# GLA levels of a hybrid encoder: both directions side by side, one 512-column instruction for two of 256

## The chip, the cores and the metric

The kernel runs on one core of a Trainium2 chip. The metric is the device time of one execution in microseconds (us), as the median of several runs. Five engines work side by side, each through its own queue in order: PE multiplies matrices (PEld loads its weights), DVE, ACT and POOL work element by element on up to 128 partitions, and SP issues DMA transfers.

## The reference

One layer over a prompt of 512 tokens and a sample of 1024. The input projection feeds four mixers and a gate; the change touches the first mixer, gated linear attention (GLA), which runs in both directions over the tokens:

```python
def gla_chunked(q, k, v, g, strict):
    # o_t = sum_{s<=t (s<t if strict)} (q_t * prod_{r=s+1..t} a_r) . k_s  v_s
    ...
def gla_branch(q, k, v, lr, wg2_f, bg_f, wg2_b, bg_b, onorm_g):
    ...
    o_f = gla_chunked(q, k, v, log_gate(lr_f, wg2_f, bg_f), strict=False)
    o_b = flip(gla_chunked(flip(q), flip(k), flip(v), flip(log_gate(lr_b, wg2_b, bg_b)), strict=True))
    o = rms_norm(o_f + o_b, onorm_g)
def hybrid_layer(x, c, ...):
    h = rms_norm(x, pre_g) * (1 + scale[:, None, :]) + shift[:, None, :]
    proj = h @ w_in
    ...
    out_a = gla_branch(a_q, a_k, a_v, a_lr, ...)
    out_b = fnet_branch(b_u, fnet_w)
    out_c = attention_branch(c_q, c_k, c_v, q_norm_g, k_norm_g)
    out_d = sgu_branch(d_u, d_v, sgu_norm_g, sgu_w, sgu_b)
    mixed = jnp.concatenate([out_a, out_b, out_c, out_d], axis=-1) * jax.nn.silu(z)
    y = rms_norm(mixed @ w_out, post_g)
    return x + gate[:, None, :] * y
```

Here `a_r` is the forget gate, the exponential of `g`. There are 4 heads with 32 key columns and 64 value columns each.

## The kernel before

The tokens are handled in three groups of 512: group 2 is the prompt, groups 0 and 1 are the sample. All large matrix products take float32 values split into a high and a low part (`h` and `l`) and add three products (high by high, high by low, low by high), in the helper `mms` (L86). The split is always an ACT cast for the high part and a subtraction (L98) for the low one.

For each group GLA begins in `gla_in` (L711). The queries `aq` and keys `ak` lie as 128 rows (4 heads by 32) by 512 tokens. For each direction d a gate `f` of 128 by 512 is made: DVE L736, a POOL subtraction L98, an ACT exponential L738. Then `gla_pass1` (L762) works in seven levels, m = 1, 2, 4, ..., 64. Inside each block of 2m tokens, the level couples the one half's queries to the other half's keys: forward (`qpi`, `ksx`) the second half's queries to the first half's keys, backward (`qsi`, `kpx`) the other way round. Each level from m = 2 on splits half the columns of each of the four tiles, two pieces of 256 columns each into `kh`, `kl`, `qh`, `ql` (ACT L797 and L803, POOL L98 for `kl`, DVE L98 for `ql`), makes 48 small matmuls (L815, 32 rows by 128 columns), and takes the scores into `st` through a mask (DVE L820, `copy_predicated`). Behind that every level multiplies half the columns by the gate products of the half block: the two query halves on POOL, the two key halves on DVE (at m = 1 POOL multiplies the keys and DVE copies the other half, L841 and L842), and DVE forms the next level's gate products `ntf` and `ntb` out of pairs. The tile `st` is cleared by POOL (L785) before the first level writes it. The buffers `kh`, `kl`, `qh`, `ql` are double, so a level's operands can be ready one level ahead of PE.

The order of each engine's queue is set when the program is built, by a scheduler that simulates readiness and takes priorities. Wide matrix products of later stages (input projections of the other mixers) serve as filling work on PE. A level's first matmul is held back by hand until so many thousand columns of filling work are placed before it: `LEVEL_AT` (L42) gives, for each group, the start and the step, and L808 to L816 apply it. After the levels, `st` is split (`sth` on ACT L861, `stl` on DVE) and multiplied by the values.

Names of other stages that share the engines: `wt`, `wr`, `parts` are weights being split and passed through memory (L298, L306), `bev` (L953), `dvu` (L446), `kev` (L498) and `cev` (L507) are projections taken out of PSUM, `rp_t`, `rope` and the small `rs_` tiles (L124 to L134) belong to the norm and rotation of attention's queries and keys, `zr` is the gate path.

Of the kernel before, what the change touches and what calls it, by code (L numbers as in the profile page):

```python
# [39 lines left out]
LEVELS = (1, 2, 4, 8, 16, 32, 64)  # L40
# [5 lines left out]
def hybrid_encoder(  # L46
# [7 lines left out]
    V, S, G, T = nc.vector, nc.scalar, nc.gpsimd, nc.tensor  # L54
# [656 lines left out]
    def gla_in(pool, g, o4):  # L711

        aq = pool.tile([128, 512], F32, tag="aq", bufs=1, name="aq")
# [10 lines left out]
        lrT = pool.tile([96, 512], F32R, tag="qh", bufs=2, name="lrT")  # L724
        V.tensor_copy(lrT, lr)
        sub(V, lrT[32:64, :], lr[32:64, :], lrT[32:64, :])
        ff = []
        for d in range(2):
            pl = ps_s()
            T.matmul(pl, w2t[d], lrT, start=True, stop=True)  # L730
            t = pool.tile([128, 512], F32, tag="ql", bufs=2, name="gt_a")
            S.activation(t, pl, AF.Abs, bias=bg[:, d:d + 1])
            S.activation(t, t, AF.Exp, scale=-1.0)
            S.activation(t, t, AF.Ln, bias=1.0)
            f = pool.tile([128, 512], F32, tag=f"f{d}", bufs=1, name=f"f{d}")
# [15 lines left out]
        prod = pool.tile([128, 512], F32, tag="ksx", bufs=1, name="prod")  # L751
        mul(G, prod, aq, ak)
        pd = ps_o()
        for b in range(4):
# [6 lines left out]

    def gla_pass1(pool, ppool, g, blk0, ap_all, u_f, u_b, aq, ak, vhl, ff, avx):  # L762

        qpi = ppool.tile([128, 512], F32, tag=f"qpi{g}", bufs=1, name=f"qpi{g}")
        qsi = ppool.tile([128, 512], F32, tag=f"qsi{g}", bufs=1, name=f"qsi{g}")
        ksx = pool.tile([128, 512], F32, tag="ksx", bufs=1, name="ksx")
        mul(V, qpi, aq, ff[0])
        mul(V, qsi, aq, ff[1])

        prod = pool.tile([128, 512], F32, tag="kpx", bufs=1, name="prod2")  # L770
        for i, src in enumerate((qsi, qpi)):
            qv, kv, pv = (t.rearrange("p (n two) -> p two n", two=2) for t in (src, ak, prod))
            mul(G, pv[:, i], qv[:, i], kv[:, 1 - i])
# [9 lines left out]
        kpx = pool.tile([128, 512], F32, tag="kpx", bufs=1, name="kpx")  # L783
        st = pool.tile([128, 4, 4, 128], F32, tag="st", bufs=1, name="st")
        G.memset(st, 0.0)  # L785
        tf, tb = ff
        ntot = 512
        def halves(t, m):
            v = t.rearrange("p (n two m) -> p n two m", two=2, m=m)
            return v[:, :, 0, :], v[:, :, 1, :]  # L790

        def level(li, m):
            kh = pool.tile([128, 512], F32R, tag="kh", bufs=2, name="kh")
            kl = pool.tile([128, 512], F32R, tag="kl", bufs=2, name="kl")
            for i, src in enumerate((ksx, kpx)):
                s_, h_, l_ = halves(src, m)[i], halves(kh, m)[i], halves(kl, m)[i]
                S.copy(h_, s_)  # L797
                sub(G, l_, s_, h_)
            qh = pool.tile([128, 512], F32R, tag="qh", bufs=2, name="qh")
            ql = pool.tile([128, 512], F32R, tag="ql", bufs=2, name="ql")  # L800
            for i, src in enumerate((qsi, qpi)):
                s_, h_, l_ = halves(src, m)[i], halves(qh, m)[i], halves(ql, m)[i]
                S.copy(h_, s_)  # L803
                sub(V, l_, s_, h_)

            pts = [ps_s(), ps_s(), ps_s(), ps_o()]
            last = None
            at, step = LEVEL_AT[g]  # L808
            for i, (k, q) in enumerate(((kh, qh), (kh, ql), (kl, qh))):
                for b in range(4):  # L810
                    c = slice(b * 128, (b + 1) * 128)
                    for h in range(4):
                        r = slice(32 * h, 32 * h + 32)
                        with tc.issue_after(last.ins) if last is not None else after_columns(at + (li - 1) * step):
                            last = T.matmul(pts[h][:, c], k[r, c], q[r, c], start=i == 0 and b == 0, stop=i == 2,  # L815
                                            skip_group_check=True)  # L816
            for h in range(4):
                ptv = pts[h].rearrange("p (b t) -> p b t", b=4)
                if m < 64:
                    V.copy_predicated(st[:, h], mk[:, li - 1, :].unsqueeze(1).to_broadcast([128, 4, 128]), ptv)  # L820
                else:
                    S.copy(st[0:64, h, :, 64:128], ptv[0:64, :, 64:128])
                    S.copy(st[64:128, h, :, 0:64], ptv[64:128, :, 0:64])

        for li, m in enumerate(LEVELS):
            if m > 1:
                level(li, m)
            n2 = ntot // 2
            tfv, tbv = (t.rearrange("p (n two) -> p n two", two=2) for t in (tf, tb))

            def bc(t, i):
                return t[:, :, i].unsqueeze(2).to_broadcast([128, n2, m])

            q1, q2 = halves(qpi, m)
            mul(G, q2, q2, bc(tfv, 0))
            q1, q2 = halves(qsi, m)
            mul(G, q1, q1, bc(tbv, 1))
            if m == 1:
                k1, k2 = halves(ak, 1)
                mul(G, halves(ksx, 1)[0], k1, bc(tfv, 1))  # L840
                V.tensor_copy(halves(ksx, 1)[1], k2)  # L841
                V.tensor_copy(halves(kpx, 1)[0], k1)  # L842
                mul(G, halves(kpx, 1)[1], k2, bc(tbv, 0))
            else:
                k1, k2 = halves(ksx, m)
                mul(V, k1, k1, bc(tfv, 1))
                k1, k2 = halves(kpx, m)
                mul(V, k2, k2, bc(tbv, 0))
            ntf = pool.tile([128, n2], F32, tag=f"tf{n2}", bufs=1, name="ntf")
            ntb = pool.tile([128, n2], F32, tag=f"tb{n2}", bufs=1, name="ntb")  # L850
# [443 lines left out]
    with later():  # L1294
        t = [[], [], []]
# [110 lines left out]
```

## Time and profile before

| | |
|---|---|
| median of 3 runs | 1240.02 us (1235.35 to 1246.15) |
| the profiled execution | 1240.43 us, its span 1238.6 us |
| mean granted TensorE clock | 0.943 of full speed |
| busy, share of the span | PE 89%, DVE 61%, ACT 48%, POOL 31% |

The span is the stretch that the trace covers; the profiled execution's own time is 1.8 us longer. Times of single instructions below come from that execution. A row of the timeline reads: start, duration, engine, line, operation, output and inputs, shape, count, and in brackets the idle time of the engine just before it and what ended it.

### The profile page before, as it was taken

The numbers are of one execution on the slowest core, as the hardware profiler recorded it, in microseconds if no ns is written. First come the engines' busy times: TensorE is split into PE (matmuls) and PEld (weight loads), VectorE is DVE, ScalarE is ACT, GpSimd is POOL, SyncE is SP. The second block draws the span as 40 slices with busy tenths as digits, with TensorE's granted clock in tenths as the row PEclk, the third lists the DMA queues.
The fourth block names the chain that finished last, engine by engine and source line by source line (L and its number), as shares of the span: only waits on it lengthen the run. The fifth ranks groups of instructions, "written<-read, shape, count | busy, mean of one in ns | idle before, by whom it ended". The sixth has DMA issues, their size and how long they took to land. (4 is left out here: it accounts for less than half of the span.)

```text
span 1238.6 us, 21385 instructions
## 1 busy us (share of the span) xinstructions
PE 1105.1 (89%) x7906; PEld 973.3 (79%) x7906; DVE 754.5 (61%) x1440; ACT 597.3 (48%) x1472; POOL 382.0 (31%) x372
## 2 busy tenths in 40 slices
PE   5998779998999888998898899788989999988995
PEld 1587768764999886767898778588989998977995
DVE  6439776647454299552239852774787568686615
ACT  4334246643565235462123244444675667666623
POOL 3136654561011147113016510553141011223003
PEclk9999798998999998999999789789999999999998
DMA  8497656877433765576765346678347333264272
GB/s 316 159 324 243 227 183 202 309 271 234 150 117 116 239 198 159 173 251 199 250 203 168 112 147 194 197 252 282 128 145 247 111 103 94 81 212 130 82 252 97
DMA packets 126393, 233.99 MB, mean 189 GB/s; under 512 B 13092, under 2 KB 65796, under 8 KB 126288
## 3 DMA queue, kind: packets, MB, share of 16 engines
q1 hardware_dynamic: 121624, 227.49, 56.0%
q10 hardware_dynamic: 4664, 5.13, 1.2%
q8 instruction: 62, 1.02, 0.3%
q14 instruction: 43, 0.35, 0.1%
HBM read 162.97 MB, written 69.61 MB: 188 GB/s over the span
## 5 line engine op out<-in xcount | busy, mean ns | idle before, releaser
L86 PE MATMUL ps_mm<-wt,oph 128*128 128x256 f32 x2240 | 443.2, 293 | 20.7 <-DMA wt<-parts 11.0
L86 PEld LDWEIGHTS ps_mm<-wt,oph 128*128 128x128 f32 x2240 | 368.6, 199 | 30.6 <-DMA wt<-parts 11.3
L86 PE MATMUL ps_mm<-wt,opl 128*128 128x256 f32 x1120 | 326.0, 292 | 0.0
L86 PEld LDWEIGHTS ps_mm<-wt,opl 128*128 128x128 f32 x1120 | 222.0, 199 | 1.8
L86 PE MATMUL ps_mm<-oph,wt 128*128 128x512 f32 x576 | 194.8, 410 | 12.7 <-DMA wt<-parts 6.1
L554 DVE TENSOR_REDUCE nm<-ps_s 128x1 f32<-128x512 f32 x160 | 108.9, 686 | 58.6 <-PE ps_s L553 57.8
L86 PEld LDWEIGHTS ps_mm<-oph,wt 128*128 128x128 f32 x576 | 112.8, 197 | 38.9 <-ACT kh L797 3.8
L98 DVE TENSOR_TENSOR ptl<-ps_t,pth 128x512 fp32r<-128x512 f32 x160 | 108.4, 685 | 56.7 <-ACT pth L571 56.2
L98 POOL TENSOR_TENSOR wt<-wr,wt 128x512 fp32r<-128x512 f32 (+1 forms) x68 | 90.4, 1333 | 140.5 <-ACT wt L306 131.9
L571 ACT CAST pth<-ps_t 128x512 fp32r<-128x512 f32 x160 | 91.2, 590 | 65.8 <-PE ps_t L569 64.8
L561 ACT ACTIVATE pr<-ps_s,nm 128x512 f32<-128x512 f32 x160 | 109.5, 692 | 20.9 <-DVE nm L557 16.2
L86 PE MATMUL ps_mm<-opl,wt 128*128 128x512 f32 x288 | 117.9, 409 | 0.0
L569 PE MATMUL ps_t<-cs,pr 128*128 128x128 f32 x640 | 91.6, 276 | 1.1 <-DVE nm L557 0.6
L306 ACT CAST wt<-wr 128x512 fp32r<-128x512 f32 (+1 forms) x80 | 47.6, 597 | 77.5 <-PE ps_mm L86 36.0
L569 PEld LDWEIGHTS ps_t<-cs,pr 128*128 128x128 f32 x640 | 76.3, 143 | 9.5 <-PE ps_s L553 1.0
L101 POOL TENSOR_TENSOR oc<-oc,den 128x256 f32<-128x256 f32 x24 | 14.8, 629 | 220.3 <-DVE oc L104 199.0
L86 PEld LDWEIGHTS ps_mm<-opl,wt 128*128 128x128 f32 x288 | 56.7, 197 | 11.4
L552 PE MATMUL ps_s<-kT,qT 128*128 128x512 f32 x128 | 56.5, 442 | 5.0 <-ACT pr L561 4.8
L98 POOL TENSOR_TENSOR opl<-m,oph 128x512 fp32r<-128x512 f32 x30 | 39.1, 1319 | 52.6 <-ACT oph L1086 52.6
L553 PE MATMUL ps_s<-kT,qT 128*128 128x512 f32 x128 | 51.3, 401 | 0.0
L101 POOL TENSOR_TENSOR yt<-yt,gp 128x512 f32<-128x512 f32 x20 | 25.9, 1293 | 81.9 <-ACT jk L1118 64.8
L86 PE MATMUL ps_o<-pth,vkv 128*128 128x256 f32 x256 | 41.7, 285 | 0.6 <-DVE nm L557 0.6
(349 smaller groups left out, 2112.6 us busy)
## 6 DMA issues: line engine op xcount, KB each, us to landing
wt<-parts SPq DMA_DIRECT2D x136, 512.0 KB, 3.6
parts<-wt SPq DMA_DIRECT2D x68, 512.0 KB, 4.7
wr<-wp SPq DMA_DIRECT2D x48, 256.0 KB, 3.8
adar<-ada SPq DMA_DIRECT2D x16, 512.0 KB, 6.0
zT<-zr SPq DMA_DIRECT2D x30, 256.0 KB, 2.8
zt<-zT SPq DMA_DIRECT2D x30, 256.0 KB, 5.0
mt<-mixd SPq DMA_DIRECT2D x24, 256.0 KB, 5.2
wr<-wo SPq DMA_DIRECT2D x20, 256.0 KB, 4.5
```

Source lines behind the costliest of these rows:

```text
L86: t = T.matmul(out, a, b, start=first and i == 0, stop=last and i == len(terms) - 1, skip_group_check=skip)
L98: e.tensor_tensor(out, a, b, ALU.subtract)
L101: e.tensor_tensor(out, a, b, ALU.mult)
L306: (V.tensor_copy if part_engine(HIGH_V, u, S) is V else S.copy)(h, raw)
L552: T.matmul(sp, qT[:, h, qc], kT[kv][:, kc], start=True, stop=False)
L553: T.matmul(sp, qT[:, h, qc], kT[2 + kv][:, kc], start=False, stop=True)
L554: V.tensor_reduce(nm[:, f:f + 1], sp, AX, ALU.max, negate=True)
L561: S.activation(pr, sps[f], AF.Exp, bias=nm[:, 0:1], accum_out=rsum[:, b, h, f:f + 1])
L569: T.transpose(pt[:, k * 128:(k + 1) * 128], pr[f][:, k * 128:(k + 1) * 128], ident)
L571: S.copy(pth[f][:, :, qc], ptv)
```

## The change

Queries, keys and gates of both directions now lie side by side: `q2` and `k2` are tiles of 1152 columns (backward in the first 512, forward in the next), and `ff` holds three gate rows of 512 (backward, forward, backward again), for which ACT makes one exponential more per group. Views (`cross`, `pair`, `factor`) pick the halves of a level in both directions at once, so that each cast, subtraction and multiplication of a level is one instruction of 512 columns. The gate products of a level are one instruction of three rows. At m = 1 the keys are first copied in both directions by one ACT instruction of 1024 columns, and the multiplication of the keys moves from POOL to DVE. The first product of queries and gates becomes one DVE instruction of 1024 columns. `prod` gets a buffer of its own. The matmuls, `st`, and everything behind the levels stay.

```diff
-        ff = []
+        ff = pool.tile([128, 3, 512], F32, tag="ff", bufs=1, name="ff")
...
-            f = pool.tile([128, 512], F32, tag=f"f{d}", bufs=1, name=f"f{d}")
+            f = ff[:, 1 - d, :]
             V.tensor_scalar(f, pl, bg[:, d:d + 1], 0.0, ALU.add, ALU.min)
             sub(G, f, f, t)
+            if d:
+                S.activation(ff[:, 2, :], f, AF.Exp, scale=1.0 / 16.0)
             S.activation(f, f, AF.Exp, scale=1.0 / 16.0)
...
-        mul(V, qpi, aq, ff[0])
-        mul(V, qsi, aq, ff[1])
+        q2 = ppool.tile([128, pad], F32, tag=f"q2{g}", bufs=1, name=f"q2{g}")
+        k2 = pool.tile([128, pad], F32, tag="k2", bufs=1, name="k2")
+        qsi, qpi, ksx, kpx = q2[:, 0:512], q2[:, 512:1024], k2[:, 0:512], k2[:, 512:1024]
+        def cross(t, m):
+            v = t[:, 0:2 * (512 + m)].rearrange("p (i c) -> p i c", i=2)[:, :, 0:512]
+            return v.rearrange("p i (n two m) -> p i n two m", two=2, m=m)[:, :, :, 0, :]
+        def pair(t, m):
+            return t.rearrange("p (n two m) -> p two n m", two=2, m=m)
+        mul(V, q2[:, 0:1024].rearrange("p (i c) -> p i c", i=2), aq.unsqueeze(1).to_broadcast([128, 2, 512]), ff[:, 0:2, :])
...
+        S.copy(k2[:, 0:1024].rearrange("p (i c) -> p i c", i=2), ak.unsqueeze(1).to_broadcast([128, 2, 512]))
...
-            for i, src in enumerate((ksx, kpx)):
-                s_, h_, l_ = halves(src, m)[i], halves(kh, m)[i], halves(kl, m)[i]
-                S.copy(h_, s_)
-                sub(G, l_, s_, h_)
+            S.copy(pair(kh, m), cross(k2, m))
+            sub(G, pair(kl, m), cross(k2, m), pair(kh, m))
...
-            for i, src in enumerate((qsi, qpi)):
-                s_, h_, l_ = halves(src, m)[i], halves(qh, m)[i], halves(ql, m)[i]
-                S.copy(h_, s_)
-                sub(V, l_, s_, h_)
+            S.copy(pair(qh, m), cross(q2, m))
+            sub(V, pair(ql, m), cross(q2, m), pair(qh, m))
...
-            mul(G, q2, q2, bc(tfv, 0))
...
-            mul(G, q1, q1, bc(tbv, 1))
-            if m == 1:
-                mul(G, halves(ksx, 1)[0], k1, bc(tfv, 1))
-                V.tensor_copy(halves(ksx, 1)[1], k2)
-                V.tensor_copy(halves(kpx, 1)[0], k1)
-                mul(G, halves(kpx, 1)[1], k2, bc(tbv, 0))
...
-            mul(V, ntf, tfv[:, :, 0], tfv[:, :, 1])
-            mul(V, ntb, tbv[:, :, 0], tbv[:, :, 1])
+            mul(G, cross(q2, m), cross(q2, m), factor(0))
+            mul(V, cross(k2, m), cross(k2, m), factor(ntot))
+            mul(V, ng.rearrange("p (d n) -> p d n", d=3), gv[:, :, :, 0], gv[:, :, :, 1])
```

The queues are written anew by the scheduler. Three places are shown.

DVE at the start of group 2, before: the first product, the gate products of both directions in turn, the keys of m = 2 (`ksx`), and the other direction's keys (`kpx`) only behind them.

```order
L101 TENSOR_TENSOR qpi_4941<-aq,f_4904 128x512
L101 TENSOR_TENSOR ntf<-f_4904 128x256
L101 TENSOR_TENSOR qsi_4942<-aq,f_4914 128x512
...
L98 TENSOR_TENSOR ql<-qpi_4941,qh 128x128x2
L101 TENSOR_TENSOR ksx<-ksx,ntf 128x128x2
L101 TENSOR_TENSOR ntb<-ntb 128x4
L855 COPY tfin_5431<-ntf 128x4
L842 COPY kpx<-ak 128x256
L98 TENSOR_TENSOR ql<-qsi_4942,qh 128x128x2
L101 TENSOR_TENSOR av<-av,own_4954 128x1024
```

The same place after the change, where `k_4942` is the tile `k2` and `q_4941` the tile `q2`:

```order
L101 TENSOR_TENSOR k_4942<-k_4942,ff 128x2x256
L101 TENSOR_TENSOR q_4941<-aq,ff 128x1024
L101 TENSOR_TENSOR ng<-ff 128x768
L98 TENSOR_TENSOR wt<-wr,wt 128x512
L101 TENSOR_TENSOR ng<-ng 128x384
L101 TENSOR_TENSOR k_4942<-k_4942,ng 128x2x128x2
...
L845 COPY tfin_5375<-ng 128x8
L98 TENSOR_TENSOR ql<-q_4941,qh 128x2x128x2
```

The keys of both directions for m = 1 now come first of all, and those of m = 2 as the sixth instruction.

POOL at the same place, before, from the first multiplication of the keys to the low parts that level m = 2 needs:

```order
L101 TENSOR_TENSOR ksx<-ak,f_4904 128x256
L101 TENSOR_TENSOR prod_4946<-qpi_4941,ak 128x256
L101 TENSOR_TENSOR prod_4946<-qsi_4942,ak 128x256
L101 TENSOR_TENSOR qpi_4941<-qpi_4941,f_4904 128x256
L98 TENSOR_TENSOR kl<-ksx,kh 128x128x2
L101 TENSOR_TENSOR qsi_4942<-qsi_4942,f_4914 128x256
L101 TENSOR_TENSOR qpi_4941<-qpi_4941,ntf 128x128x2
L101 TENSOR_TENSOR kpx<-ak,f_4914 128x256
L98 TENSOR_TENSOR wt<-wr,wt 128x512
L101 TENSOR_TENSOR qsi_4942<-qsi_4942,ntb 128x128x2
L98 TENSOR_TENSOR kl<-ksx,kh 128x64x4
L98 TENSOR_TENSOR kl<-kpx,kh 128x128x2
```

And after:

```order
L98 TENSOR_TENSOR kl<-k_4942,kh 128x2x128x2
L101 TENSOR_TENSOR prod_4944<-q_4941,ak 128x256 x2
L101 TENSOR_TENSOR q_4941<-q_4941,ff 128x2x256
L98 TENSOR_TENSOR kl<-k_4942,kh 128x2x64x4
L98 TENSOR_TENSOR wt<-wr,wt 128x512 x2
```

The low part of the keys for m = 2, the last of twelve rows before, is the first now.

ACT at the start of group 1, before: the exponentials, two casts of `ksx`, then the copies of `kev`, and the query casts ahead of the second pair of them.

```order
L738 ACTIVATE f_8030<-f_8030 128x512
L738 ACTIVATE f_8040<-f_8040 128x512
L797 CAST kh<-ksx 128x128x2
L797 CAST kh<-ksx 128x64x4
L498 COPY kev<-ps_mm 128x256 x2
L397 ACTIVATE rp_t_4510<-kev 128x256
L803 CAST qh<-qpi_8067 128x128x2
L803 CAST qh<-qsi_8068 128x128x2
L498 COPY kev<-ps_mm 128x256 x2
```

And after, from the first key cast on:

```order
L802 CAST kh<-k_7954 128x2x128x2
L498 COPY kev<-ps_mm 128x256 x2
L397 ACTIVATE rp_t_4510<-kev 128x256
L802 CAST kh<-k_7954 128x2x64x4
L498 COPY kev<-ps_mm 128x256 x2
L124 ACTIVATE rs_l<-ropess,eps 128x4
L397 ACTIVATE rp_t_4548<-kev 128x256
L126 ACTIVATE rs_y<-rs_l 128x4
L124 ACTIVATE rs_l<-ropess,eps 128x4
L126 ACTIVATE rs_y<-rs_l 128x4
L806 CAST qh<-q_7953 128x2x128x2
```

The copies of `kev` now stand ahead of the second key cast, and the query cast stands behind the logarithms `rs_l`. On PE the order of the wide products is nearly the same; level m = 2 stands 1.5 thousand columns of filling work later than before in group 2, 6.7 thousand earlier in group 0, and 2.6 thousand later in group 1.

## Rows read from the trace of the kernel before

**Rows 1.** The page: engines over the whole span, and PE's 512-column matmuls (mean ns).

```profile
PE 1105.1 (89%) x7906; PEld 973.3 (79%) x7906; DVE 754.5 (61%) x1440; ACT 597.3 (48%) x1472; POOL 382.0 (31%) x372
...
L86 PE MATMUL ps_mm<-oph,wt 128*128 128x512 f32 x576 | 194.8, 410 | 12.7 <-DMA wt<-parts 6.1
```

**Rows 2.** Windows over the three GLA starts: busy time by engine, PE clock, DMA.

```profile
100.00:137.00 37.00, 24.74 (x196) 22.72 (x196) 35.51 (x56) 15.26 (x33) 28.65 (x26) 0.82 0.64 213
448.00:480.00 32.00, 22.87 (x160) 19.72 (x159) 31.79 (x57) 14.21 (x33) 25.70 (x23) 0.88 0.46 141
660.00:692.00 32.00, 26.09 (x236) 24.70 (x235) 29.79 (x61) 9.03 (x29) 23.46 (x27) 0.82 0.39 118
```

**Rows 3.** Timeline of PE, start of group 2: the instructions behind a wait.

```profile
121.62 0.33 PE L815 MATMUL ps_s<-qh,kh 32*128 32x128 f32 x3 [1.19 <-ACT kh L797]
...
126.97 0.48 PE L815 MATMUL ps_s<-qh,kl 32*128 32x128 f32 x3 [3.77 <-POOL kl L98]
...
133.31 0.51 PE L86 MATMUL ps_mm<-vhl,wsh 128*128 128x256 f32 x2 [1.79 <-ACT bev L953]
...
136.79 0.77 PE L86 MATMUL ps_mm<-wt,oph 128*128 128x256 f32 x2 [2.50 <-DVE dvu L446]
```

**Rows 4.** Timeline of PE, start of group 0: the instructions behind a wait.

```profile
464.57 0.47 PE L86 MATMUL ps_mm<-oph,wt 128*128 128x512 f32 x1 [3.79 <-DMA wt<-parts]
...
476.38 0.48 PE L815 MATMUL ps_s<-qh,kl 32*128 32x128 f32 x3 [3.19 <-POOL kl L98]
...
479.48 0.79 PE L86 MATMUL ps_mm<-oph,wt 128*128 128x512 f32 x1 [1.97 <-DVE zr L101]
```

**Rows 5.** Timeline of PE, start of group 1: the instructions behind a wait.

```profile
669.38 0.50 PE L86 MATMUL ps_mm<-wt,oph 128*128 128x256 f32 x2 [2.17 <-ACT kev L498]
...
683.72 0.43 PE L815 MATMUL ps_s<-qh,kh 32*128 32x128 f32 x1 [3.74 <-DVE st L820]
```

**Rows 6.** Timeline of POOL, group 2: the first low part of level m = 16.

```profile
141.84 0.74 POOL L98 TENSOR_TENSOR kl<-ksx,kh 128x256 fp32r<-128x256 f32 x1 [4.80 <-PE ps_o L815]
```

**Rows 7.** Groups by line and form, DVE and POOL (busy us, mean ns).

```profile
L98 DVE TENSOR_TENSOR ptl<-ps_t,pth 128x512 fp32r<-128x512 f32 x160 | 108.4, 685 | 56.7 <-ACT pth L571 56.2
L98 DVE TENSOR_TENSOR ql<-qpi,qh 128x256 fp32r<-128x256 f32 x18 | 7.4, 413 | 0.0
L101 DVE TENSOR_TENSOR ntf<-ntf 128x8 f32<-128x8 f32 x3 | 0.5, 158 | 0.0
...
L101 POOL TENSOR_TENSOR prod<-aq,ak 128x512 f32<-128x512 f32 x3 | 3.9, 1290 | 10.5 <-PE ps_mm L86 10.5
```

**Rows 8.** Timeline of ACT and POOL, group 2: last exponential, and the latest low part.

```profile
109.87 0.63 ACT L738 ACTIVATE f<-f 128x512 f32<-128x512 f32 x1 [0.92 <-POOL f L98]
...
125.10 1.81 POOL L98 TENSOR_TENSOR kl<-kpx,kh 128x256 fp32r<-128x256 f32 x1
```

**Rows 9.** Timeline of POOL and DVE, group 0: a small DVE instruction beside a long one.

```profile
445.70 2.56 POOL L98 TENSOR_TENSOR f<-f,gt_a 128x512 f32<-128x512 f32 x2 [11.24 <-ACT gt_a L734]
...
445.76 1.27 DVE L130 SCALAR_TENSOR_TENSOR rs_a<-rs_y 128x8 f32<-128x8 f32 x1
```

**Rows 10.** Timeline of SP, group 0: the DMA queue around the weights.

```profile
463.52 0.37 SPq L509 DMA_DIRECT2D qd<-cev  x1
463.98 5.52 SPq L298 DMA_DIRECT2D wt<-parts  x3
```

**Rows 11.** Timeline of ACT and POOL, group 1: the cast before `kev`, and clearing `st`.

```profile
668.38 0.40 ACT L797 CAST kh<-ksx 128x256 fp32r<-128x256 f32 x1 [5.88 <-DVE ksx L101]
...
677.93 1.81 POOL L785 MEMSET st<- 128x2048 f32 x1
```

**Rows 12.** Windows of 5 us behind the waits: columns as in Rows 2.

```profile
140.00:145.00 5.00, 5.00 (x50) 4.88 (x47) 3.37 (x7) 1.42 (x4) 1.85 (x3) 0.56 0.65 212
685.00:690.00 5.00, 5.00 (x55) 4.53 (x55) 4.47 (x9) 1.43 (x4) 2.39 (x4) 0.50 0.36 121
```

**Rows 13.** Timeline of PE behind group 2's levels: the longest wait there.

```profile
185.26 0.42 PE L867 MATMUL ps_o<-vhl,stl 128*128 128x64 f32 x1 [4.62 <-DVE stl L98]
```

More of the change, by code (lines that the diff above doesn't have):

```diff
@@ L750, in gla_in @@
             sub(V, vhl[:, b, :, 1, :], pv, vhl[:, b, :, 0, :])
-        prod = pool.tile([128, 512], F32, tag="ksx", bufs=1, name="prod")
+        prod = pool.tile([128, 512], F32, tag="prod", bufs=1, name="prod")
         mul(G, prod, aq, ak)
@@ L762, in gla_pass1 @@
     def gla_pass1(pool, ppool, g, blk0, ap_all, u_f, u_b, aq, ak, vhl, ff, avx):
-        qpi = ppool.tile([128, 512], F32, tag=f"qpi{g}", bufs=1, name=f"qpi{g}")
-        qsi = ppool.tile([128, 512], F32, tag=f"qsi{g}", bufs=1, name=f"qsi{g}")
-        ksx = pool.tile([128, 512], F32, tag="ksx", bufs=1, name="ksx")
-        mul(V, qpi, aq, ff[0])
-        mul(V, qsi, aq, ff[1])
-        prod = pool.tile([128, 512], F32, tag="kpx", bufs=1, name="prod2")
-        for i, src in enumerate((qsi, qpi)):
-            qv, kv, pv = (t.rearrange("p (n two) -> p two n", two=2) for t in (src, ak, prod))
-            mul(G, pv[:, i], qv[:, i], kv[:, 1 - i])
+        pad = 2 * 512 + 2 * LEVELS[-1]
+        q2 = ppool.tile([128, pad], F32, tag=f"q2{g}", bufs=1, name=f"q2{g}")
[7 more added lines that the diff above has]
+        mul(V, q2[:, 0:1024].rearrange("p (i c) -> p i c", i=2), aq.unsqueeze(1).to_broadcast([128, 2, 512]), ff[:, 0:2, :])
+        prod = pool.tile([128, 512], F32, tag="prod", bufs=1, name="prod2")
+        for i in range(2):
+            mul(G, pair(prod, 1)[:, i], cross(q2, 1)[:, i], pair(ak, 1)[:, 1 - i])
+        S.copy(k2[:, 0:1024].rearrange("p (i c) -> p i c", i=2), ak.unsqueeze(1).to_broadcast([128, 2, 512]))
         pd = ps_o()
@@ L782, in gla_pass1 @@
         add(V, o4, o4, avx)
-        kpx = pool.tile([128, 512], F32, tag="kpx", bufs=1, name="kpx")
         st = pool.tile([128, 4, 4, 128], F32, tag="st", bufs=1, name="st")
         G.memset(st, 0.0)
[L786 to L790, printed above, removed]
+        gt, ntot = ff.rearrange("p d c -> p (d c)"), 512
         def level(li, m):
@@ L828, in gla_pass1, with factor @@
             n2 = ntot // 2
[L829 to L834, printed above, removed]
-            mul(G, q2, q2, bc(tfv, 0))
-            q1, q2 = halves(qsi, m)
-            mul(G, q1, q1, bc(tbv, 1))
-            if m == 1:
-                k1, k2 = halves(ak, 1)
-                mul(G, halves(ksx, 1)[0], k1, bc(tfv, 1))
-                V.tensor_copy(halves(ksx, 1)[1], k2)
-                V.tensor_copy(halves(kpx, 1)[0], k1)
-                mul(G, halves(kpx, 1)[1], k2, bc(tbv, 0))
[L844 to L850, printed above, removed]
-            mul(V, ntf, tfv[:, :, 0], tfv[:, :, 1])
-            mul(V, ntb, tbv[:, :, 0], tbv[:, :, 1])
-            tf, tb, ntot = ntf, ntb, n2
+            def factor(base):
+                v = gt[:, base + 1:base + 2 * ntot - 1].rearrange("p (i c) -> p i c", i=2)[:, :, 0:ntot - 1:2]
+                return v.unsqueeze(3).to_broadcast([128, 2, n2, m])
+            mul(G, cross(q2, m), cross(q2, m), factor(0))
+            mul(V, cross(k2, m), cross(k2, m), factor(ntot))
+            ng = pool.tile([128, 3 * n2], F32, tag=f"ng{n2}", bufs=1, name="ng")
+            gv = gt.rearrange("p (d n two) -> p d n two", d=3, two=2)
+            mul(V, ng.rearrange("p (d n) -> p d n", d=3), gv[:, :, :, 0], gv[:, :, :, 1])
+            gt, ntot = ng, n2
         tfin = ppool.tile([128, 2, 4], F32, tag=f"tfin{g}", bufs=1, name=f"tfin{g}")
-        V.tensor_copy(tfin[:, 0, :], tf)
-        V.tensor_copy(tfin[:, 1, :], tb)
+        V.tensor_copy(tfin.rearrange("p d n -> p (d n)"), gt[:, 4:12])
         for b in range(4):
```

2 lines of the change are left out of this document (removed).

## The prediction

> **What bounds the kernel now.** I read the page first: PE is busy 89% of the span and no other engine over 61% [rows 1], so a faster DVE or POOL pays only where PE stands waiting for them. The chain of work that ended last covers only the final few microseconds and says nothing of the levels. So I looked, with windows of busy time, at the three stretches in which a group's GLA begins. There the picture turns: PE is busy 24.74 of 37, 22.87 of 32 and 26.09 of 32 us, idle 27.3 us in sum, while DVE is busy 35.51, 31.79 and 29.79 us and POOL 28.65, 25.70 and 23.46 [rows 2]. DVE has next to no gap in the first two: in these 101 us it is the bound, with POOL behind it, and ACT has room (38.5 us of work).
>
> Then PE's timeline, for the instructions that stand behind a wait and what ended it. In group 2: 1.19 us for ACT's `kh`, 3.77 for POOL's `kl`, 1.79 for `bev`, 2.50 for `dvu` [rows 3]; sum 9.25. In group 0: 3.19 for `kl` and 1.97 for `zr`, sum 5.16, and ahead of them 3.79 for a DMA of weights [rows 4]. In group 1: 2.17 for `kev` and 3.74 for `st`, sum 5.91 [rows 5]. The waits that GLA's own steps can cause come to 9.25 + 5.16 + 5.91 = 20.3 us; that is the most that shorter steps could take away directly.
>
> Later levels aren't part of it. From level m = 16 of group 2 on, POOL stands 4.80 us waiting for PE to give the buffer of the low part back [rows 6]: the operands are there before PE is. Whatever the change saves per step there costs and gains nothing.
>
> **The change part by part.** First the steps by themselves. A DVE subtraction of 256 columns takes 0.413 us where nothing holds it, one of 512 takes 0.685 [rows 7]; two become one, so 2 x 0.413 - 0.685 = 0.14 us saved. The key multiplication has the same form. On POOL a subtraction of 256 columns takes 0.74 [rows 6] and one 512 instruction 1.29 [rows 7]; 2 x 0.74 - 1.29 = 0.19 saved. In the stretch where PE waits, two or three levels are made: DVE saves some 5 x 0.14 = 0.7 on keys and queries and about 1.0 on gate products (seven instructions fewer, the small ones at 0.158 [rows 7], less a third row); the two copies at m = 1 go and a 512-column multiplication comes, about even. POOL saves 5 x 0.19, and its two key multiplications at m = 1 (2 x 0.74) go to DVE: 2.4 us. ACT pays one more exponential of 0.63 [rows 8] and a copy of 1024 columns, at most twice that, and saves 0.2 on each pair of casts; it has room, except that the extra exponential stands in the chain, 0.63 us. So the work itself shrinks by only 1.7 us on DVE and 2.4 on POOL per group. If that were all, the gain would be some 5 us.
>
> The larger term is the order. Before, the two directions are made one after the other, and the second direction's `kl` of level m = 2 is the twelfth POOL row; it started at 125.10 and took 1.81 [rows 8], and PE waited for it until 126.97 [rows 3]. After, it is the first row. I replayed the queues by hand with the durations above and half a microsecond of holds per two instructions (an estimate).
>
> Group 2: before, the second exponential ended at 109.87 + 0.63 = 110.5 [rows 8], the third one will at 111.1; `k2` is multiplied at 111.8, cast at 112.4, `kl` done at 114.4; the two `prod` and the query multiplication (0.74, 0.74, 1.29 and some 0.6 of holds) end at 117.8, the query cast at 118.4, `ql` at 119.2. PE came to this level at 121.62 - 1.19 = 120.4, and the level now stands 1.5 thousand columns later; a 512-column matmul takes 0.41 us [rows 1], 0.8 per thousand columns, so 1.2 us later, 121.6. That is 2.4 us of margin: the 1.19 and the 3.77 go, 4.96 us. What stood behind the late key cast on ACT (`bev`) and behind DVE's late keys (`dvu`) moves up too, but these have work of their own ahead of them: of 1.79 + 2.50 I take 1.5. Gain 6.5, bounds 3 and 9.25.
>
> Group 0: `kl` is no longer last; by the same replay the operands of m = 2 are ready at about 467.5 instead of 476.3. PE reaches the level earlier as well: PE ran out at 476.38 - 3.19 = 473.2 [rows 4], two thirds through the level, which so began at about 472; 6.7 thousand columns are 5.4 us, so it will begin at 466.5. A wait of about 1 us stays, and about 1 of the 1.97 for `zr`. Gain 3, bounds 0 and 5.16. The 3.79 for weights stays: SP issues that load only behind a store of `cev` at 463.52 [rows 10], which ends a chain of attention's rotation on DVE that the change doesn't touch.
>
> Group 1: `kev` was copied late because ACT stood 5.88 us in a cast of `ksx` [rows 11] that came ahead of it; now the copy is ahead of that cast, and the 2.17 goes. The 3.74 for `st` came from POOL clearing the tile at 677.93 [rows 11] behind the steps of both directions; these are fewer, and the level stands 2.6 thousand columns later (2.1 us). I take 2.3 of it. Gain 4.5, bounds 1 and 5.91.
>
> Sum of the three: 6.5 + 3 + 4.5 = 14.0, bounds 4 and 20.3.
>
> The clock: right after these waits PE is busy without a gap and yet at a granted clock of 0.56 and 0.50 of full speed [rows 12], the lower of the two levels most of the time; at full speed these 10 us would be 5.3. If half of that comes back with fewer gaps, it is 2.3 us; I take 2, bounds 0 and 4.7.
>
> What is late next: PE arriving earlier waits longer for what doesn't come earlier. Behind group 2's levels it already waits 4.62 us for `stl` [rows 13], which stands on DVE behind the rotation, and in group 0 the 3.79 for weights. I let a quarter of 16.0 be given back there: 12.0 remain. Against the profiled execution's own 1240.4 that is 1228.4, and since this run lies 0.4 from the median, **1228 us** for the median too.
>
> **The rivals.** (a) *Given back.* The starts get shorter, but the waits behind them take it: the rotation and the weights are on DVE and SP, PE arrives 6.5 us sooner at `stl` and waits 6.5 more; group 0's gain goes into the 3.79. Then only group 1's 4.5 and the clock's 2 or less remain: 1234 to 1240. For it: both waits exist already [rows 4, 13]. Against it: DVE, which carries the rotation, loses 1.7 us of work and a good part of its holds.
>
> (b) *Slower: longer POOL instructions hold DVE.* DVE and POOL hold each other: a DVE instruction on 8 columns, the like of which takes 0.158 alone [rows 7], took 1.27 at 445.76, until the first of two POOL subtractions of 512 columns that began at 445.70 was through [rows 9]. POOL's pieces go from 0.74 to 1.29, so a small instruction that meets one can lose 0.55 more, and norm and rotation are chains of small ones. With some 18 POOL instructions per start, each of them costing the chain 0.55, the operands come 9.9 us later than in my replay. PE would wait 7.5 in group 2 (margin 2.4), 10.9 in group 0 and 8.1 in group 1 (margin about 1.8, where the query cast now stands behind `rs_l`, the logarithms of the norm), 26.5 us against the 4.96 + 5.16 + 5.91 = 16.0 of before: 10.5 slower, **1251 us**. It turns from gain to loss where the delay d gives (d - 2.4) + (1 + d) + (d - 1.8) = 16.0, at 6.4 us per start, 0.36 for each POOL instruction. For it: rows 9, and that a step now waits for the later direction. Against it: the POOL time in total falls, so fewer instructions are met.
>
> The Trainium skill bears on this (SBUF — State Buffer, "Who interferes with whom"): a DVE instruction with two SBUF inputs and a GpSimd instruction that reads SBUF exclude each other, and the loser is blocked for the whole instruction. By that rule the hold per meeting grows as in (b), the trace agrees (1.27 us for 8 columns), and the worst case would be the 1251; but the rule also makes the total hold follow POOL's total time, which falls, and by that the sum stays at 1228.
>
> (c) *More.* All 20.3 us of waits go and the clock gives back 4.7, nothing is lost on the way: 1215. For it: the margins in groups 2 and 1. Against it: `zr`, `dvu` and `bev` depend on other work.
>
> **How the numbers follow.** My forecast, 1221 to 1234: 0.47. Given back, 1234 to 1241: 0.23. More, below 1221: 0.16. Slower, above 1241: 0.14, of it 0.10 above 1252. A measurement of this kernel, whose runs spread over 11 us, can tell about 1%, so from 1227.6 to 1252.4 is no change. Faster: half of the forecast and all of (c), 0.24 + 0.16, about 0.41. Slower by over 1%: 0.10. The rest, 0.49, is within. For 8 in 10 I leave out a part of (c) below 1216 and most of (b): 1216 to 1243.
>
> **What would show it.** In the profile after: PE's first wait at level m = 2 of group 2 under 1 us, `kl` of both directions done before 116 us after the start; in group 1 no wait for `kev`; PE idle in the three windows down from 27.3 to about 13; DVE's busy time over the whole span down by some 10 us and POOL's by some 10. Wrong in its order step: `kl` or the query cast still the last operand there. Wrong in its last step: the starts shorter by 14 us and the waits for `stl` and for weights longer by as much. Rival (b) is right if the rows of 8 columns on DVE lengthen and PE waits longer than before at m = 2 in groups 0 and 1.

## The result and the profile after

The changed kernel takes 1230.39 us (median of 20 runs, 1225.05 to 1239.32) against 1240.74 for the kernel before in the same batch (20 runs): a ratio of 0.9917, interval 0.99 to 0.9933, so 10.3 us less. The forecast was 1228 us in a range of 1216 to 1243. The interval does not reach 1, so the change is real, although the prediction, which allowed 1% for noise, would have called anything from 1227.6 on no change. The size was right. The way in which it comes about is mostly another one, as the traces and the experiments show.

The page of the kernel after, the line that answers to [rows 1]:

```profile
PE 1098.0 (89%) x7906; PEld 966.2 (79%) x7906; DVE 741.3 (60%) x1374; ACT 599.0 (49%) x1442; POOL 366.9 (30%) x327
```

DVE's time fell from 754.5 by 13.2 us and POOL's from 382.0 by 15.1. The span fell by 10.5 (to 1228.1), and of this only 3.4 us is idle time of PE (span less busy time: 133.5 before, 130.1 after); the other 7.1 is PE's busy time, with the same 7906 matmuls. The mean granted clock is 0.949 against 0.943.

The same three windows of the kernel after as in [rows 2]:

```profile
100.00:137.00 37.00, 24.00 (x198) 22.14 (x197) 33.86 (x41) 14.57 (x27) 23.19 (x17) 0.85 0.65 223
448.00:480.00 32.00, 23.06 (x165) 18.22 (x163) 31.07 (x47) 14.09 (x30) 21.28 (x15) 0.91 0.37 116
660.00:692.00 32.00, 28.15 (x293) 26.56 (x292) 28.41 (x53) 10.78 (x27) 21.85 (x18) 0.84 0.38 116
```

PE's idle time in them is 25.8 us, hardly less than the 27.3 of before; I had expected about 13. PE's timeline of the kernel after shows what stands there now, in place of [rows 3 to 5]:

```profile
123.40 0.33 PE L818 MATMUL ps_s<-ql,kh 32*128 32x128 f32 x3 [1.96 <-DVE ql L98]
132.12 0.80 PE L86 MATMUL ps_mm<-vhl,wsh 128*128 128x256 f32 x2 [6.12 <-ACT bev L942]
135.02 0.77 PE L86 MATMUL ps_mm<-wt,oph 128*128 128x256 f32 x2 [1.25 <-DVE dvu L446]
...
460.38 0.68 PE L86 MATMUL ps_mm<-oph,wt 128*128 128x512 f32 x1 [3.57 <-ACT cev L507]
472.32 0.50 PE L86 MATMUL ps_mm<-oph,wt 128*128 128x512 f32 x1 [2.90 <-DVE rs_a L130]
477.47 0.32 PE L818 MATMUL ps_s<-qh,kh 32*128 32x128 f32 x1 [2.13 <-DVE st L823]
...
671.25 0.33 PE L818 MATMUL ps_s<-ql,kh 32*128 32x128 f32 x3 [1.54 <-DVE ql L98]
678.65 0.29 PE L818 MATMUL ps_s<-qh,kh 32*128 32x128 f32 x1 [1.76 <-DVE st L823]
```

The waits for `kh`, `kl` and `kev` are gone, as forecast. In group 2 the 3.77 us for `kl` went into 6.12 for `bev`. The timelines of DVE, POOL and ACT of the kernel after tell how, here in the order of time:

```profile
111.15 1.52 POOL L98 TENSOR_TENSOR kl<-k,kh 128x512 fp32r<-128x512 f32 x1 [2.48 <-ACT kh L802]
...
118.31 4.23 DVE L101 TENSOR_TENSOR ng<-ng 128x192 f32<-128x192 f32 x5
...
119.77 2.53 POOL L98 TENSOR_TENSOR wt<-wr,wt 128x512 fp32r<-128x512 f32 x2
...
122.66 0.69 DVE L98 TENSOR_TENSOR ql<-q,qh 128x512 fp32r<-128x512 f32 x1
...
127.50 1.80 POOL L796 MEMSET st<- 128x2048 f32 x1 [2.40 <-DVE ap_allq L104]
...
129.27 1.15 POOL L101 TENSOR_TENSOR q<-q,ng 128x512 f32<-128x512 f32 x1
...
130.45 0.62 ACT L806 CAST qh<-q 128x512 fp32r<-128x512 f32 x1 [4.17 <-POOL q L101]
...
131.49 0.57 ACT L942 COPY bev<-ps_mm 128x512 f32<-128x512 f32 x1
```

`kl` of both directions is done at 112.7, 14 us earlier than before. But DVE comes through its row no faster: five gate products of 192 columns and fewer take 4.23 us beside POOL instructions of 512 columns. The low part of the queries, `ql`, stands behind them and is done at 123.35, where the replay had 119.2: so PE waits 1.96 us at level m = 2, where the forecast had 2.4 us of margin and said under 1. POOL's clearing of `st` waits for DVE (the values `av` lie in the same buffer, tag `st`), the query multiplication stands behind the clearing, ACT's query cast waits for it, and the copy of `bev` stands behind that cast. One late operand was taken away, and PE waits for the next thing that comes through DVE.

Wider windows, over each group's GLA with its levels, first of the kernel before, then of the one after:

```profile
100.00:205.00 105.00, 84.56 (x779) 79.53 (x779) 77.69 (x137) 46.64 (x116) 60.93 (x59) 0.85 0.61 207
430.00:525.00 95.00, 84.41 (x693) 72.13 (x692) 75.44 (x144) 41.88 (x96) 43.91 (x46) 0.95 0.57 179
640.00:765.00 125.00, 113.85 (x882) 102.29 (x881) 79.56 (x160) 45.28 (x119) 44.13 (x47) 0.89 0.52 163
```

```profile
100.00:205.00 105.00, 84.80 (x773) 80.08 (x772) 72.95 (x115) 45.81 (x105) 54.10 (x44) 0.85 0.61 203
430.00:525.00 95.00, 84.72 (x674) 71.35 (x673) 67.19 (x112) 43.54 (x86) 36.70 (x27) 0.95 0.53 171
640.00:765.00 125.00, 115.71 (x904) 103.29 (x904) 73.14 (x136) 49.08 (x117) 39.50 (x32) 0.93 0.55 173
```

DVE works 19.4 us less in sum (232.7, then 213.3) and POOL 18.7 less. Over the whole span it is 13.2 and 15.1: the same stretch of time doesn't hold quite the same work in both kernels. By groups of instructions, DVE's time fell in GLA's own steps alone. The key multiplications behind m = 1, before and then after:

```profile
L101 DVE TENSOR_TENSOR ksx<-ksx,ntf 128x256 f32<-128x256 f32 x18 | 13.3, 738 | 0.0
L101 DVE TENSOR_TENSOR kpx<-kpx,ntb 128x256 f32<-128x256 f32 x18 | 13.2, 736 | 1.2 <-POOL kl L98 1.2
```

```profile
L101 DVE TENSOR_TENSOR k<-k,ng 128x512 f32<-128x512 f32 x18 | 15.4, 853 | 0.1
```

Two of them took 1.47 us before, one of 512 columns takes 0.85: 0.62 saved, not 0.14. Summed over all of GLA's level steps on DVE, first products and copies included, the durations that the trace lists fall from 74.6 us (132 instructions) to 52.6 (66). Those of the other 1308 rise from 749.5 to 756.1. (Listed durations overlap a little, so they add up to more than the busy time.)

To place the gain I compared when each trace has issued the same share of all wide matmul columns. The kernel after is ahead by 1.3 us at 100, by 0.8 at 205 (so nothing in group 2), by 1.6 at 410 and 4.1 at 525 (2.5 around group 0), by 4.0 at 655 and 10.3 at 765 (6.3 around group 1), and by 10.6 at the end. These are two single executions. Of group 1's 6.3, 1.9 is idle time of PE (125 - 113.85 = 11.2 before, 9.3 after), and a further part is the clock. The stretch of group 1's levels, before and then after:

```profile
670.00:740.00 70.00, 62.77 (x549) 56.09 (x548) 53.06 (x102) 24.13 (x64) 31.19 (x36) 0.80 0.39 123
```

```profile
670.00:740.00 70.00, 63.12 (x543) 55.65 (x544) 46.01 (x83) 25.99 (x58) 24.93 (x22) 0.88 0.43 136
```

From 670 to 740 the granted clock is 0.80 before and 0.88 after, 5.6 us of full speed in 70. Over all executions the difference is smaller but there: the mean granted clock is 0.947 in the 20 of the changed kernel and 0.941 in the 35 of the kernel before that ran beside the last experiments.

### The profile page after: what moved, and what is told of

It reads as the page before. It is cut to its first block, busy times and chain, and to the rows that moved or that the text cites. A ratio compares the mean times of both kernels' runs of the same rounds, so it can differ in the third digit from the quotient of the medians.

```text
span 1228.1 us, 21246 instructions
## 1 busy us (share of the span) xinstructions
PE 1098.0 (89%) x7906; PEld 966.2 (79%) x7906; DVE 741.3 (60%) x1374; ACT 599.0 (49%) x1442; POOL 366.9 (30%) x327
## 5 line engine op out<-in xcount | busy, mean ns | idle before, releaser
L86 PEld LDWEIGHTS ps_mm<-oph,wt 128*128 128x128 f32 x576 | 110.3, 193 | 40.9 <-DMA wt<-parts 5.1
```

What stands on the lines that cost most here:

```text
L86: t = T.matmul(out, a, b, start=first and i == 0, stop=last and i == len(terms) - 1, skip_group_check=skip)
```

## The experiments

Each ran beside the kernel before on the same chip; ratios are to it, with 95% intervals. The first four ask which part carries the gain. Theory 1 is the forecast's main step, that the order of the operands does.

**Steps split again.** In the changed kernel, for `kh` and `kl` (and alike for `qh`, `ql` and the two multiplications):

```diff
-            S.copy(pair(kh, m), cross(k2, m))
-            sub(G, pair(kl, m), cross(k2, m), pair(kh, m))
+            for i in range(2):
+                S.copy(pair(kh, m)[:, i], cross(k2, m)[:, i])
+                sub(G, pair(kl, m)[:, i], cross(k2, m)[:, i], pair(kh, m)[:, i])
```

> The tiles lie side by side as in the changed kernel, the third gate row, the copied keys, the key multiplication of m = 1 on DVE and the merged gate products stay; but each cast, subtraction and multiplication of a level is again two instructions of 256 columns, one for each direction. Theory 1 (the gain is the new order of the queues: both directions' keys first, the copies of kev ahead of the second key cast): nearly all of the gain stays, 1230 to 1233 us. Theory 2 (the gain is the shorter work of the merged steps, fewer instructions on DVE and POOL): most of it goes, 1236 to 1241 us. Theory 3 (any new order would have moved the time as much, by luck): anywhere from 1228 to 1245.

Measured: 1233.31 us, 0.9929 (0.9903 to 0.9955). Most of the gain is there without merging a single level step. Merging them is worth 0.9917 / 0.9929 = 0.9988, 1.5 us, not separated from nothing. The bulk sits in what else the change brought. The page of this kernel:

```profile
PE 1104.0 (89%) x7906; PEld 973.6 (79%) x7906; DVE 747.3 (61%) x1413; ACT 602.6 (49%) x1478; POOL 377.3 (31%) x366
```

So 6.0 us more busy time on DVE than in the changed kernel and 10.4 more on POOL go with these 1.5 us (between 2 less and 5 more, by the intervals).

**Gate products merged alone**, in the kernel before (for which both gates `f` and both gate products lie in one tile each):

```diff
...
-            mul(V, ntf, tfv[:, :, 0], tfv[:, :, 1])
-            mul(V, ntb, tbv[:, :, 0], tbv[:, :, 1])
...
+            ng = pool.tile([128, 2, n2], F32, tag=f"ng{n2}", bufs=1, name="ng")
+            mul(V, ng, gv[:, :, :, 0], gv[:, :, :, 1])
...
```

> The kernel before with one edit: the gate products of both directions are one instruction of two rows (seven DVE instructions for fourteen in each group), all else in two halves as before. Theory 1: the late key steps of the second direction stay late, so the time stays within 2 us of before, 1238.5 to 1242. Theory 2: some 2 us less DVE work at each of three starts, of which a third to a half arrives, 1236 to 1238. Theory 3: 1230 to 1246.

Measured: 1240.34 us, 0.9997 (0.9972 to 1.0022). Nothing by itself, though DVE's busy time in the profiled execution is 4.2 us shorter than before (750.3).

**Keys of m = 1 back on POOL**, in the changed kernel:

```diff
-            mul(V, cross(k2, m), cross(k2, m), factor(ntot))
+            mul(G if m == 1 else V, cross(k2, m), cross(k2, m), factor(ntot))
```

> The changed kernel with the key multiplication of m = 1 back on POOL, one instruction of 512 columns. Theory 1: every key step of both directions starts behind a POOL instruction of 1.3 us and more instead of a DVE one of 0.7, and the low part of the keys queues behind it: 1 to 2 us at each start, 1232 to 1236. Theory 2: DVE loses 0.7 and POOL gains 1.3 per group, so no change that can be measured, 1229.5 to 1232. Theory 3: 1226 to 1240.

Measured: 1233.58 us, 0.9938 (0.9912 to 0.9964). As theory 1 said, but the interval holds the 0.9917 of the unedited kernel too: not decided.

**A buffer of its own for `st`**, in the changed kernel:

```diff
-        st = pool.tile([128, 4, 4, 128], F32, tag="st", bufs=1, name="st")
+        st = pool.tile([128, 4, 4, 128], F32, tag="sc", bufs=1, name="st")
```

> The changed kernel with a buffer of its own for st, so that POOL may clear it without waiting for DVE's sum over av; the queues of PE, DVE and ACT are the same to the row, POOL's differ only in where the clearing stands. Theory 1, with the step that failed: in group 2 PE's 6.12 us wait for bev comes from ACT's query cast, which waits for POOL's multiplication, which stood behind a clearing that waited 2.40 for DVE; without it that wait falls to 2 to 4 us and the one for st in groups 0 and 1 (2.13 and 1.76) goes: 1223 to 1227. Theory 2: no work is removed, 1229.5 to 1231.5. Theory 3: 1225 to 1236.

Measured: 1228.07 us, 0.9886 (0.9859 to 0.9913). PE's timeline of this kernel, the row that answers to the 6.12:

```profile
131.28 0.80 PE L86 MATMUL ps_mm<-vhl,wsh 128*128 128x256 f32 x2 [3.70 <-ACT bev L942]
```

The wait fell to 3.70 with the queues of PE, DVE and ACT unchanged, so the clearing's place was 2.4 us of it: that chain is shown. The waits for `st` in groups 0 and 1 stayed (2.13 and 2.54), against the expectation, and 0.9886 isn't separated from 0.9917.

The next four test the order directly. Before, `prod2` lay in the buffer of `kpx`, so `kpx` could be written only once PE had read `prod2`. The change gave `prod` a buffer of its own in passing. Theory 1b says that this made the gain.

**A buffer of its own for `prod`**, in the kernel before:

```diff
-        prod = pool.tile([128, 512], F32, tag="ksx", bufs=1, name="prod")
+        prod = pool.tile([128, 512], F32, tag="prod", bufs=1, name="prod")
...
-        prod = pool.tile([128, 512], F32, tag="kpx", bufs=1, name="prod2")
+        prod = pool.tile([128, 512], F32, tag="prod", bufs=1, name="prod2")
```

> The kernel before with one edit: prod and prod2 get a buffer of their own, instead of those of ksx and kpx. Nothing is merged and nothing lies side by side. Theory 1b (what made the second direction's keys late was that kpx may be written only when PE has read prod2 out of the same buffer; the change freed it in passing, and that is most of the gain): 1231 to 1234 us, and PE's 3.77 us wait for kl in group 2 gone. Theory 1a (the gain is in the side-by-side layout and the keys made by DVE and ACT, which put both directions first): 1238 to 1241. Theory 2 (shorter merged steps): 1240.

Measured: 1240.4 us, 0.9996 (0.9972 to 1.0019). PE's timeline of this kernel in group 2 has no wait for `kh` or `kl` left, and these two at the place:

```profile
133.00 0.79 PE L86 MATMUL ps_mm<-vhl,wsh 128*128 128x256 f32 x2 [6.24 <-ACT bev L953]
136.62 0.77 PE L86 MATMUL ps_mm<-wt,oph 128*128 128x256 f32 x2 [1.97 <-DVE dvu L446]
```

This is the experiment on which the larger part of the forecast's main step falls. The operand for which PE waited longest was made early, and 1.19 + 3.77 + 1.79 + 2.50 = 9.25 us of waits became 6.24 + 1.97 = 8.2. The wide window of this kernel over group 2 (same columns):

```profile
100.00:205.00 105.00, 84.96 (x771) 80.42 (x772) 76.50 (x136) 46.28 (x115) 60.21 (x59) 0.84 0.61 203
```

PE's idle time there is 20.0 us; it was 20.4. DVE's 76.50 and POOL's 60.21 are nearly those of before (77.69 and 60.93). In group 0 the wait for `kl` is gone too. In group 1 the wait for `kev` stays (1.53 us), so that part of the order isn't tested by this kernel.

**`prod` in the buffer of `k2`**, in the changed kernel, so that the keys of both directions are made late (the first `prod`, in `gla_in`, moves there too):

```diff
...
-        prod = pool.tile([128, 512], F32, tag="prod", bufs=1, name="prod2")
+        prod = pool.tile([128, pad], F32, tag="k2", bufs=1, name="prod2")[:, 0:512]
...
-        S.copy(k2[:, 0:1024].rearrange("p (i c) -> p i c", i=2), ak.unsqueeze(1).to_broadcast([128, 2, 512]))
...
+        k2 = pool.tile([128, pad], F32, tag="k2", bufs=1, name="k2")
+        qsi, qpi, ksx, kpx = q2[:, 0:512], q2[:, 512:1024], k2[:, 0:512], k2[:, 512:1024]
+        S.copy(k2[:, 0:1024].rearrange("p (i c) -> p i c", i=2), ak.unsqueeze(1).to_broadcast([128, 2, 512]))
```

> The changed kernel with the opposite edit: prod and prod2 lie in the buffer of k2, so the keys of both directions may be copied only when PE has read prod2. All merged steps stay. Theory 1b: the gain goes, or more, since now both directions wait: 1238 to 1246 us, with PE waiting some 4 us for the low part of the keys at level m = 2. Theory 1a and theory 2: 1230 to 1233.

Measured: 1224.52 us, 0.9876 (0.9839 to 0.9913), the fastest of all, where theory 1b expected the gain to go. PE's timeline of this kernel in group 2:

```profile
125.59 0.50 PE L86 MATMUL ps_mm<-vhl,wsh 128*128 128x256 f32 x2 [2.30 <-ACT bev L942]
128.59 0.48 PE L818 MATMUL ps_s<-qh,kl 32*128 32x128 f32 x3 [0.55 <-POOL kl L98]
```

Here the scheduler put the product that needs `bev` ahead of level m = 2 instead of behind it: 2.30 us for `bev` instead of 6.12, 0.55 for `kl`. The late operand cost next to nothing here, where the queue had been written for it.

**The buffer for `st`, in the kernel before**, the same edit as above:

> The kernel before with a buffer of its own for st alone. If the clearing of st costs PE time in the kernel before as well (3.74 us for st in group 1): 1235 to 1238 us. Theory 1b (before, PE waits for the late keys first, and POOL clears beside that): 1238 to 1241.

Measured: 1240.28 us, 1.0005 (0.9982 to 1.0028). Nothing.

**Both buffers, in the kernel before**, nothing merged:

> The kernel before with both buffers, for prod and for st, and nothing merged. Theory 1b: both gains, 1228 to 1231 us, so the merged steps would be worth some 1 us or nothing. Theory 2: no more than 2 us below before, 1238 to 1240.

Measured: 1238.09 us, 0.9969 (0.9948 to 0.9991): 3.8 us, more than the 2 that theory 2 allows, though the median lies in its range, and far from theory 1b's. Theory 1b falls, and theory 1 for the most part: with both buffers free and nothing merged, the kernel before gives somewhat over a third of the gain at best estimate (1 to 6 us by the interval).

What all five kernels with the side-by-side tiles had in common, beside the tiles, was less busy time on DVE (735.7 to 747.3 us) and POOL (366.9 to 377.3). Of the last four, one takes such work away, one joins two buffers, and two add such work.

**Key copies of m = 1 on ACT**, in the kernel before:

```diff
-                V.tensor_copy(halves(ksx, 1)[1], k2)
-                V.tensor_copy(halves(kpx, 1)[0], k1)
+                S.copy(halves(ksx, 1)[1], k2)
+                S.copy(halves(kpx, 1)[0], k1)
```

> The kernel before with one edit: the two key copies of m = 1 on ACT instead of DVE (0.28 and 0.95 us on DVE, three groups). In the runs so far the medians follow DVE's busy time over the whole span (735.7 us with 1224.5, 741.3 with 1230.4, 750.3 with 1240.3, 758.7 with 1238.1), and buffers and rows that moved the keys earlier did nothing alone. Theory 4 (DVE is the bound of the starts; what leaves its time, its own or what POOL makes it wait, comes off the span at some 0.75): 3.7 us less on DVE, 1237 to 1239. Theory 5 (the gain belongs to the layout with both directions in one tile as a whole): 1239.5 to 1242.

Measured: 1236.51 us, 0.9978 (0.9954 to 1.0002): 2.7 us less, where theory 4 said 2.8; just not separated from nothing. In the profiled execution DVE is busy 6.2 us less than before (748.3).

**`prod` in `k2` and a buffer for `st`**, both in the changed kernel:

> The changed kernel with prod in the buffer of k2 (which gave 1224.5) and a buffer of its own for st (which gave 1228.1) together. Theory 4: each had made DVE's busy time 4 to 6 us shorter; together 1221 to 1224. If both work by the same waits: 1224 to 1226.

Measured: 1228.43 us, 0.9915 (0.989 to 0.994). The two don't add, against theory 4; it is no better than the changed kernel, although DVE's 735.3 us in its profiled execution are the fewest of all.

**First product on DVE three times**, in the changed kernel:

```diff
-        mul(V, q2[:, 0:1024].rearrange("p (i c) -> p i c", i=2), aq.unsqueeze(1).to_broadcast([128, 2, 512]), ff[:, 0:2, :])
+        for _ in range(3):
+            mul(V, q2[:, 0:1024].rearrange("p (i c) -> p i c", i=2), aq.unsqueeze(1).to_broadcast([128, 2, 512]), ff[:, 0:2, :])
```

> The changed kernel with the first product of queries and gates on DVE written three times (two more instructions of 1024 columns and 1.23 us for each group, 7.4 us in all; the value is the same). Theory 4: 7.4 x 0.75 = 5.5 us, 1234 to 1238. Theory 5 or 3 (order, not DVE's time): 1229 to 1233.

Measured: 1239.93 us, 0.9995 (0.997 to 1.002). Over the changed kernel that is 0.9995 / 0.9917 = 1.0079, 9.7 us (6 to 13 by the intervals): the whole gain is gone. The page of this kernel, and the three wide windows:

```profile
PE 1105.8 (89%) x7906; PEld 970.6 (78%) x7906; DVE 751.1 (61%) x1380; ACT 600.7 (49%) x1442; POOL 370.0 (30%) x327
...
100.00:205.00 105.00, 88.33 (x784) 82.27 (x783) 77.54 (x119) 47.75 (x108) 55.45 (x46) 0.85 0.61 204
430.00:525.00 95.00, 81.43 (x660) 68.97 (x659) 70.84 (x116) 37.39 (x75) 39.03 (x30) 0.93 0.54 168
640.00:765.00 125.00, 112.56 (x908) 101.53 (x907) 77.09 (x142) 48.42 (x119) 40.73 (x32) 0.92 0.54 169
```

The 7.4 us are what the added instructions take alone; DVE's busy time rose by 9.8 us (741.3 to 751.1). It doesn't cost the same everywhere: PE's idle time in the three windows is 16.7, 13.6 and 12.4 us, in the changed kernel 20.2, 10.3 and 9.3, so in group 2 PE waits less than without the added work.

**POOL's `prod2` three times**, in the changed kernel:

```diff
-        for i in range(2):
+        for i in (0, 1) * 3:
             mul(G, pair(prod, 1)[:, i], cross(q2, 1)[:, i], pair(ak, 1)[:, 1 - i])
```

> The changed kernel with the two POOL multiplications of prod2 made three times (four more instructions of 256 columns for each group, 0.74 us alone, 9 us in all; the value is the same). Theory 4: POOL is not the bound by itself, but it makes DVE wait; some 2 to 5 us, 1232 to 1236, with DVE's busy time up by as much though it got no work. If POOL's time doesn't reach DVE or PE: 1229 to 1232.

Measured: 1244.45 us, 1.0043 (1.0017 to 1.0069), by the ratios 15.6 us over the changed kernel (12 to 19 by the intervals) for 9 us of POOL work, more than theory 4 said. The page of this kernel:

```profile
PE 1109.0 (89%) x7906; PEld 975.2 (79%) x7906; DVE 748.6 (60%) x1374; ACT 599.0 (48%) x1442; POOL 381.2 (31%) x339
```

DVE has the same 1374 instructions as the changed kernel and is busy 748.6 us instead of 741.3. POOL itself is 14.3 us longer. That the 7.3 us are POOL's doing is likely but not shown alone: the queues are in another order here, and among the kernels with these 1374 instructions and no added POOL work DVE's busy time goes from 735.3 to 741.3.

## Why the prediction was right, and where not

**The bound.** Partly shown. That DVE, with POOL holding it, is the bound of the starts agrees with the two kernels with added work: 9.7 us of time where DVE was 9.8 longer, 15.6 where POOL was 14.3 longer, about one for one. But both additions, the first product and `prod2`, stand at the head of GLA, so they also make every later operand late. An engine with no room left and a longer chain of operands weren't tried apart. Busy time alone doesn't decide it. Steps split again gave DVE 6.0 us and POOL 10.4 more for 1.5 us of time, gate products merged took 4.2 off DVE for nothing, and in group 2 the added product cost PE no idle time. What was taken away in the kernel before (the copies, 2.7 us) isn't clear of nothing.

**The steps by themselves.** "So the work itself shrinks by only 1.7 us on DVE and 2.4 on POOL per group": this term was mis-sized. Over the span DVE's busy time fell by 13.2 us and POOL's by 15.1, 4.4 and 5.0 per group; the sign "down by some 10" for each was nearer. I counted the durations of instructions that nothing holds. The pairs of key multiplications took 1.47 us and not 0.83, so merging them saved 0.62 and not 0.14. It doesn't follow that this made the gain. The merged level steps, after which the change is named, carry 1.5 us of it at best estimate (0.9988). The rest is with what the kernel with the split steps keeps: the first product, the keys of m = 1 taken from POOL, the copies taken from DVE, the gate products, the buffer for `prod`, and the order that came with them. I can't divide it among these: in the kernel before, the copies alone gave 2.7, the gate products and the buffer alone nothing.

**The order.** "The larger term is the order" failed. The queue moved as described, `kl` was early (done 112.7, replay 114.4), the waits for `kl` and `kev` went, and group 2 gained nothing by it. With the `kl` waits of groups 2 and 0 taken away alone (own buffer for `prod`) the ratio was 0.9996, with the keys late again (`prod` in `k2`) 0.9876. The wait for `kev` was not taken away alone. In the terms of the sum: group 2, forecast 6.5, gave none; the waits of 9.25 became 1.96 + 6.12 + 1.25 = 9.3. Group 0, forecast 3, gave about 2.5 in this pair of traces, with PE's idle time the same (95 - 84.41 = 10.6 and 10.3), so not by the step I named. Group 1, forecast 4.5, gave 6.3, of which 1.9 is idle time. I had said that what stood behind the late cast on ACT, `bev`, "moves up too": it went the other way, behind a query cast that waits for POOL's clearing. The replay left out the five gate products ahead of `ql` on DVE, which turned 2.4 us of margin into a wait of 1.96. It followed the operands of one level and stopped there; nothing in it followed the queues to the next reader.

**The clock.** The term of 2 was low in this pair: PE's busy time fell by 7.1 us with the same matmuls, and 670 to 740 alone accounts for 5.6 of full speed. But the mean clock also differs between single executions of kernels with other times (0.945 where the first product was made three times, 0.952 with the copies on ACT), so a pair of traces can't settle it. All executions together give an estimate: 0.947 against 0.941 on average, and among the 35 of the kernel before an execution is some 7 us shorter for each 0.01 of clock. That makes some 4 to 5 us of the 10.3 go along with the clock, about the upper bound of the term (4.7). Whether the clock is their cause or follows from fewer gaps, no run shows.

**The rivals.** "Given back" was right in that the starts hold as much idle time as before, wrong about the place: `bev`, `rs_a` and `cev` rather than `stl`, where the wait is 4.64 us and was 4.62, and the weights. "Longer POOL instructions hold DVE" agrees with the traces in its mechanism (five small products in 4.23 us beside POOL's long ones) and not in its sign: the time fell. From the rule in the Trainium skill (SBUF — State Buffer, "Who interferes with whom") the prediction had worked out that the total hold follows POOL's total time, which fell by 15.1. On DVE, GLA's level steps shrank by more than the merging explains; the other 1308 instructions did not (749.5, then 756.1), so as a whole that isn't borne out.

**The number.** 1228 for 1230.39 is in good part luck: the larger term, the order, was far too large, and what was put too small, the clock and the work by itself, seems to have made up for it.

**Open.** Why `prod` in `k2` with a buffer for `st` gives back what `prod` in `k2` alone gained (0.9915, 0.9876; the intervals overlap), and whether the 1224.52 of the latter is better than the changed kernel's 1230.39: measured in other batches, with intervals that overlap. Every edit but the buffer for `st` in the changed kernel also rewrites the queues, and PE's row of filling work with them, so a part of each result may be the place of the levels and not the edited work; that was not tried apart.

## What to carry to other kernels

Where an engine is busy without a gap in a stretch, making one operand earlier may only hand the wait to the next thing in its queue, as here. In these runs work at the head of such a stretch was dear (some 10 to 15 us for two or four more instructions per group), and work spread over its levels was cheap. Before counting on a wait's end, undo that wait alone: here an edit of one buffer's name took the longest of them away and gained nothing. If a change merges many steps, ask which of them stand where the other engine waits; the ones in the steady levels, though most in number, were worth 1.5 us at best estimate.

## What had not been expected of the hardware

The price of work on POOL: twelve more POOL instructions, 9 us alone, made POOL 14.3 us busier and the kernel some 15 us slower, and DVE was 7.3 us busier with no instruction added on it. Part of the time shows at PE: its busy time with the same 7906 matmuls was 1109.0 us there and 1098.0 in the changed kernel, 11.0 of the 12.2 us between the two spans, at mean granted clocks of 0.938 and 0.949. That execution lay low in clock, though: over all twelve the mean was 0.943, against 0.947 in the twenty of the changed kernel.
